# Prompt attention of a hybrid decoder layer: sample columns of a finished head moved into its tile and split with it, one reciprocal and one scaling step for both query tiles of a pair

## The chip, the cores and the metric

The kernel runs on one core of one Trainium2 chip. The metric is the device time of one execution in microseconds; the time quoted for a kernel is the median of its runs. Engines are named as the profile names them: PE multiplies matrices, PEld loads its weights, DVE is the vector engine, ACT the scalar engine, POOL is GpSimd, and SP issues most of the DMAs.

## The reference

One layer of a decoder with two batches at once: a prompt of 1024 new tokens, and 8 sample sequences of 8 new tokens each that attend to 4096 cached positions in pages. Both go through the same stages: a projection, attention over the 256 keys that an indexer picks, a gated recurrence (RG-LRU), a merge of the two branches, an output projection and a SwiGLU FFN. All is float32. Of the attention, per query block of 128:

```python
sel = index_topk(qi, wi, ki, pos, 256)
logits = einsum(q, k_sel) * HEAD_DIM ** -0.5 + rel_bias[rel_bucket(dist)]
p = softmax(where(valid, logits, NEG_INF))
out = einsum(p, v_sel)                       # 8 heads, 2 kv heads, head_dim 128
...
merged = sigmoid(ga) * (attn_out @ w_o_attn) + sigmoid(gb) * (lru_out @ w_o_lru)
```

## The kernel before

Every float32 product is made of three products in a faster format: an operand x is split into hi, which is x rounded to that format, and lo, which is x minus hi. The helper `split` does this with one ACT copy (L194) and one subtraction on DVE or POOL (L198); `mm3` (L181 to L183) multiplies hi by hi, lo by hi and hi by lo into one PSUM bank. The engines' instructions are not run in the order of the code: the tile framework reorders each engine's queue by its own estimate of when operands and buffers are ready, and what it built is then fixed. SP, too, has one queue in order.

The code around the change is `prompt_attention`, a generator that yields after each small step. It runs from about 835 to 1090 us of the span, in two stretches:

- **First stretch, 835 to 988 us.** The attention of the samples (`sample_attention`) runs on all engines, with K and V gathered by POOL's DMAs (L1156), transposed (L1188), copied out of PSUM by ACT and DVE as `kt` (L1190, L1192), multiplied (L1200), and so on. Between its steps the prompt attention is advanced. The flag `self.sdone` is false.
- **Second stretch, 988 to 1090 us.** The samples are done, `self.sdone` is true, and the prompt attention has the core to itself. Heads 0 to 2 and a part of head 3 fall into the first stretch, the rest of the 8 heads into the second. At its end `merge` begins, whose first product reads all heads as weights and streams through the gate of `w_o_attn`.

A head has 8 query tiles of 128 rows, t = 0 to 7, taken as four pairs m = 0 to 3 (`both`). For one tile, `stage_a` adds bias and mask of the nearest 256 keys into E (L1403, on POOL for even t and on DVE for odd t), makes the logits on PE, adds and takes the maximum on DVE out of PSUM into the tile L (L1425, then the reduction L1430), and takes the exponential of L in place on ACT with its row sums (L1431). Tile t has (t + 1) * 128 columns, so 128 to 1024. L1431 is followed by the function `norm`: the reciprocal of the row sums on DVE (L1434) and the scaling of L by it in place, on ACT in the first stretch (L1436) and on POOL in the second (L1438). `norm` isn't run at once but put into the list `nlag = Lag(1)`: the one of tile t is issued when tile t + 1 has been put.

`stage_b` of a pair transposes the scaled L of both tiles on PE (L1499), splits the transposes (`ph` on ACT, `pl` on DVE, both out of PSUM) and multiplies them with V. It is interleaved by `weave` with `both` of a later pair: of the pair two later in the first stretch (PLW) and of the pair four later in the second (PLAG). When a head is through, its output is in DRAM (`atd`), written in four pieces `ao`. In the second stretch `load_at(h)` loads it back as the tile `at` of 1024 columns and splits it into `ah` and `al`, the weights of `merge`; the 64 columns of the samples for that head lie in the constant tile `as_` and are split on their own (`split_s`) into columns 1024 to 1087 of `ah` and `al`. Head 7 isn't written out, and its sample columns are split by `split_s` before its loop. `todo` is a list of postponed steps that `do()` runs at the start of the next pair.

`m()` gives a small tile from a ring of 14. `sqrt_table` (L309) is a one-element square root into such a tile, issued by the later stage `up_init` so that ACT has the table for its square roots before it needs them (L298).

## Time and profile before

| | us |
|---|---|
| median of 3 runs | 2012.59 |
| lowest and highest | 2010.61, 2012.98 |
| the profiled execution's own time | 2007.54 |
| its span (first to last instruction) | 2005.8 |
| prompt attention in it | about 835 to 1090 |

The profile is of one execution. Its span is what the rows below are measured from: a start of 902.77 is 902.77 us after the first instruction. 1.74 us of the execution lie outside of the span. The execution was 5.05 us shorter than the median of the runs, so rows of it are used for differences, not for the level.

### The profile page before, as it was taken

The numbers are of one execution on the slowest core, as the hardware profiler recorded it, in microseconds if no ns is written. First come the engines' busy times: TensorE is split into PE (matmuls) and PEld (weight loads), VectorE is DVE, ScalarE is ACT, GpSimd is POOL, SyncE is SP. The second block draws the span as 40 slices with busy tenths as digits, with TensorE's granted clock in tenths as the row PEclk, the third lists the DMA queues.
The fourth block names the chain that finished last, engine by engine and source line by source line (L and its number), as shares of the span: only waits on it lengthen the run. The fifth ranks groups of instructions, "written<-read, shape, count | busy, mean of one in ns | idle before, by whom it ended". The sixth has DMA issues, their size and how long they took to land.

```text
span 2005.8 us, 33491 instructions
## 1 busy us (share of the span) xinstructions
PE 1934.0 (96%) x12413; PEld 1707.0 (85%) x12413; DVE 1382.7 (69%) x3084; ACT 1014.9 (51%) x1885; POOL 432.2 (22%) x366
## 2 busy tenths in 40 slices
PE   7999999999998989999889999999999999999998
PEld 5999888899997877777688999978888888878886
DVE  6454876788898666577796244596666766586796
ACT  5554688667776332477575122553333333345445
POOL 2102655000002666644474440000000000000000
PEclk9999999999999999999999999999999999999999
DMA  4633444222325998988624325313332332492543
GB/s 144 156 85 100 127 140 122 61 61 79 90 72 190 323 327 298 299 275 265 230 83 170 98 100 182 109 57 107 102 96 84 121 103 90 140 374 86 155 118 106
DMA packets 221152, 297.12 MB, mean 148 GB/s; under 512 B 20228, under 2 KB 155292, under 8 KB 220860
## 3 DMA queue, kind: packets, MB, share of 16 engines
q1 hardware_dynamic: 199484, 219.47, 34.5%
q0 software_dynamic: 21504, 75.51, 10.9%
q8 instruction: 98, 1.61, 0.4%
q14 instruction: 66, 0.54, 0.1%
HBM read 225.51 MB, written 64.28 MB: 144 GB/s over the span
## 4 chain that ended last, share of the span: by engine, by line
PE 73%; DVE 12%; ACT 6%; DMA 4%; issue 3%; POOL 0%; SPq 0%; DVEq 0%; ACTq 0%; POOLq 0%
PE mm L181 9%; PE mm L182 9%; PE mm L183 9%; PE ax L1818 5%; PE ax L1819 5%; PE ax L1820 5%; PE ax L1188 2%; PE mm L1818 2%; PE mm L1819 2%; PE mm L1820 2%; PE mm L2062 2%; PE mm L2061 2%; PE mm L2063 2%; PE ax L1200 2%; PE ax L2062 1%
## 5 line engine op out<-in xcount | busy, mean ns | idle before, releaser
L181 PE MATMUL mm<-xh,wh 128*128 128x384 f32 (+2 forms) x936 | 310.2, 331 | 0.2 <-ACT sg L966 0.2
L183 PE MATMUL mm<-xh,wl 128*128 128x384 f32 (+2 forms) x936 | 307.9, 329 | 0.7 <-POOL wl L198 0.7
L182 PE MATMUL mm<-xl,wh 128*128 128x384 f32 (+2 forms) x936 | 307.8, 329 | 0.0
L183 PEld LDWEIGHTS mm<-xh,wl 128*128 128x128 f32 (+1 forms) x936 | 175.4, 187 | 2.6 <-POOL wl L198 1.5
L181 PEld LDWEIGHTS mm<-xh,wh 128*128 128x128 f32 (+1 forms) x936 | 175.8, 188 | 1.9 <-ACT sg L966 0.7
L194 ACT ACTIVATE wh<-wr 128x1024 fp32r<-128x1024 f32 (+1 forms) x81 | 85.3, 1054 | 181.0 <-PE mm L182 87.8
L182 PEld LDWEIGHTS mm<-xl,wh 128*128 128x128 f32 (+1 forms) x936 | 175.8, 188 | 1.3
L198 POOL TENSOR_TENSOR wl<-wr,wh 128x1024 fp32r<-128x1024 f32 (+1 forms) x47 | 115.5, 2458 | 247.7 <-ACT wh L194 208.2
L1156 POOL DMA_INDIRECT g<-cache_k,c x64 | 69.4, 1085 | 333.0 <-DVE r L1030 272.3
L1818 PE MATMUL ax<-xb,wu 128*128 128x512 f32 x336 | 132.3, 394 | 2.0 <-ACT xb L194 2.0
L1819 PE MATMUL ax<-xb,wu 128*128 128x512 f32 x336 | 131.8, 392 | 0.0
L1820 PE MATMUL ax<-xb,wu 128*128 128x512 f32 x336 | 131.5, 391 | 0.0
L753 ACT ACTIVATE c<-sc,p 128x768 int8<-128x768 f32 (+2 forms) x93 | 96.4, 1037 | 12.2 <-DVE p L797 11.1
L194 ACT ACTIVATE wu<-wg 128x512 fp32r<-128x512 f32 x63 | 37.6, 627 | 94.9 <-DVE wg L1683 92.3
L194 ACT ACTIVATE ha<-hr 128x512 fp32r<-128x512 f32 x77 | 48.3, 627 | 72.7 <-PE ax L2063 30.0
L194 ACT ACTIVATE gh<-wg 128x1024 fp32r<-128x1024 f32 x44 | 46.7, 1061 | 71.0 <-PE ax L1820 37.4
L749 DVE TENSOR_SCALAR_CACHE_REDUCE c<-sc,p 128x384 uint8<-128x384 f32 (+3 forms) x102 | 78.1, 766 | 1.8
L1818 PE MATMUL mm<-xb,gh 128*128 128x512 f32 x200 | 77.9, 393 | 0.7 <-ACT gh L194 0.7
L1820 PE MATMUL mm<-xb,gl 128*128 128x512 f32 x200 | 78.1, 390 | 0.1
L1819 PE MATMUL mm<-xb,gh 128*128 128x512 f32 x200 | 78.0, 391 | 0.0
L181 PE MATMUL mm<-lh,wh 128*128 128x272 f32 x256 | 76.9, 302 | 0.0
L1818 PEld LDWEIGHTS ax<-xb,wu 128*128 128x128 f32 x336 | 63.8, 190 | 15.1 <-ACT xb L194 2.2
(500 smaller groups left out, 5775.4 us busy)
## 6 DMA issues: line engine op xcount, KB each, us to landing
wr<-w_in SPq DMA_DIRECT2D x40, 512.0 KB
hr<-hd SPq DMA_DIRECT2D x77, 256.0 KB
wg<-w_ffn_gate SPq DMA_DIRECT2D x44, 256.0 KB
wg<-w_ffn_up SPq DMA_DIRECT2D x44, 256.0 KB
wd<-w_ffn_down SPq DMA_DIRECT2D x22, 512.0 KB
hd<-hs SPq DMA_DIRECT2D x33, 256.0 KB
x<-x_prompt SPq DMA_DIRECT2D x16, 512.0 KB
wr<-w_o_lru SPq DMA_DIRECT2D x16, 512.0 KB
```

Of the source, the lines that this page charges most:

```text
L181: t.matmul(out, ah, bh, start=start, stop=False)
L182: t.matmul(out, ah, bl, start=False, stop=False)
L183: t.matmul(out, al, bh, start=False, stop=stop)
L194: nc.scalar.activation(hi, src, AF.Copy)
L198: eng.tensor_tensor(out=lo, in0=src, in1=hi.bitcast(F32), op=ALU.subtract)
L749: self.tc.keep_in_program_order(v.tensor_scalar(self.junk[:, :ap.shape[-1]], ap, th, 0.0, op0=op, op1=ALU.add, accum_out=cnt[:, r, i:i + 1]))
L753: self.tc.keep_in_program_order(nc.scalar.activation(self.junka[:, :ap.shape[-1]], ap, AF.Sign, bias=ncd[:, r:r + 1].bitcast(F32), accum_o ...
L1156: nc.gpsimd.indirect_dma_start(out=G[:, :1024], out_offset=None, in_=src, in_offset=bass.IndirectOffsetOnAxis(ap=self.ix32[:, b, c:c + 1], ...
L1818: t.matmul(ps, h[:, c], x[:, :512], start=start and k == 0, stop=False, skip_group_check=True)
L1819: t.matmul(ps, h[:, c], x[:, 512:1024], start=False, stop=False, skip_group_check=True)
L1820: t.matmul(ps, l[:, c], x[:, :512], start=False, stop=k == 3, skip_group_check=True)
L2062: t_.matmul(banks[t], s[:, c], m[:, 512:], start=False, stop=False, skip_group_check=True)
```

## The change

Three things are done. First, `load_at` loads the 64 sample columns of a head with a second DMA, out of `as_` into columns 1024 to 1087 of `at`, and one split over 1088 columns replaces the two over 1024 and 64; the split is put on `todo`, so it comes with the next `do()`. `split_s` is left for head 7 alone. Second, the row sums of a pair's two tiles are the two columns of one small tile `sm`, from a ring of its own (`sr`, 10 buffers), and `norm` is one function for the pair: one reciprocal of 128x2, then the scaling of both tiles. It is put into `nlag` once for a pair, so it is issued after the next pair's second exponential. Third, only the negated maximum still takes a tile of the ring of 14. After the heads, one more `do()` runs what is left on `todo`.

```diff
--- before.py
+++ after.py
@@ -1375,9 +1375,10 @@
         def load_at(h):
             x = self.S(name="at")
             self.dma(x[:, :TP], self.atd[h])
+            self.dma(x[:, TP:NT], self.as_[:, h, :])
+
             self.ah[h], self.al[h] = self.S(F32R, name="ah"), self.S(F32R, name="al")
-            self.split(x[:, :TP], self.ah[h][:, :TP], self.al[h][:, :TP], "s", "v")
-            split_s(h)
+            todo.append(lambda: self.split(x[:, :NT], self.ah[h][:, :NT], self.al[h][:, :NT]))
 
         def split_s(h):
             self.split(self.as_[:, h, :], self.ah[h][:, TP:NT], self.al[h][:, TP:NT])
@@ -1393,7 +1394,7 @@
 
             todo.append(fn)
 
-        def stage_a(h, t):
+        def stage_a(h, t, sm):
             qh, ql = qn[h]
             (kh, kl), _, bt = G[h // 4]
             W = (t + 1) * P
@@ -1426,23 +1427,25 @@
                                            op0=ALU.add, op1=ALU.max, accum_out=mx[:, i:i + 1])
                     i += 1
                 yield
-            nm, sm, rs = self.m(), self.m(), self.m()
+            nm = self.m()
             v.tensor_reduce(nm, mx[:, :i], axis=AX.X, op=ALU.max, negate=True)
             nc.scalar.activation(L[:, :W], L[:, :W], AF.Exp, bias=nm, accum_out=sm)
+            return L
+
+        def both(h, m):
+            sm, rs = (self.m(2, tag="sr", bufs=10) for _ in range(2))
+            La = yield from stage_a(h, 2 * m, sm[:, 0:1])
+            Lb = yield from stage_a(h, 2 * m + 1, sm[:, 1:2])
 
             def norm():
                 self.tc.keep_in_program_order(v.reciprocal(rs, sm))
-                if not self.sdone:
-                    nc.scalar.activation(L[:, :W], L[:, :W], AF.Copy, scale=rs)
-                else:
-                    nc.gpsimd.tensor_tensor(out=L[:, :W], in0=L[:, :W], in1=rs.to_broadcast([P, W]), op=ALU.mult)
+                for L, W, r in ((La, (2 * m + 1) * P, rs[:, 0:1]), (Lb, (2 * m + 2) * P, rs[:, 1:2])):
+                    if not self.sdone:
+                        nc.scalar.activation(L[:, :W], L[:, :W], AF.Copy, scale=r)
+                    else:
+                        nc.gpsimd.tensor_tensor(out=L[:, :W], in0=L[:, :W], in1=r.to_broadcast([P, W]), op=ALU.mult)
 
             nlag.put(norm)
-            return L
-
-        def both(h, m):
-            La = yield from stage_a(h, 2 * m)
-            Lb = yield from stage_a(h, 2 * m + 1)
             return h, m, La, Lb
 
         def weave(a, na, b, nb):
@@ -1545,6 +1548,7 @@
         self.mk = self.MK = None
         while ready:
             load_at(ready.pop(0))
+        do()
 
 
     def merge(self):
```

Line numbers after line 1378 are higher by 1 to 4 in the changed kernel: its reciprocal is L1441, its ACT scaling L1444, its transposes L1502, its exponential L1432.

The order of the instructions moves at three places. The first is ACT in the first stretch, around the exponential of tile 7 of head 1 (the third time in the loop of that kind: L with 1024 columns). `kt` and `run` and the L of L1233 belong to the samples. Before:

```order
L1431 ACTIVATE L_9997,m_10059<-L_9997,m_10058 128x896
L1436 ACTIVATE L_9899<-L_9899,m_9990 128x768
L1232 ACTIVATE run_10050<-run_9921,run_10049 128x1
L1233 ACTIVATE L_10046,m_10048<-L_10046,run_10049 128x512
L194 ACTIVATE ph_10078<-ax_10074 128x384
L1487 ACTIVATE ao_10089<-ax_10082 128x256
L1190 ACTIVATE kt_10118<-ax_10126 128x512
L1190 ACTIVATE kt_10119<-ax_10151 128x512
L1431 ACTIVATE L_10067,m_10145<-L_10067,m_10144 128x1024
L1436 ACTIVATE L_9997<-L_9997,m_10060 128x896
L194 ACTIVATE ph_10173<-ax_10168 128x512
L1431 ACTIVATE L_10161,m_10227<-L_10161,m_10226 128x128
```

and after the change, from the same exponential of 896 columns on:

```order
L1432 ACTIVATE L_9977,sr_9973<-L_9977,m_10038 128x896
L1232 ACTIVATE run_10030<-run_9900,run_10029 128x1
L1233 ACTIVATE L_10026,m_10028<-L_10026,run_10029 128x512
L1490 ACTIVATE ao_10065<-ax_10058 128x256
L1190 ACTIVATE kt_10094<-ax_10102 128x512
L1432 ACTIVATE L_10043,sr_9973<-L_10043,m_10120 128x1024
L1444 ACTIVATE L_9841<-L_9841,sr_9838 128x640
L1444 ACTIVATE L_9878<-L_9878,sr_9838 128x768
L1190 ACTIVATE kt_10095<-ax_10126 128x512
L1432 ACTIVATE L_10138,sr_10134<-L_10138,m_10203 128x128
L194 ACTIVATE ph_10150<-ax_10145 128x512
L194 ACTIVATE ph_10166<-ax_10161 128x512
```

The scalings of 640 and 768 columns now follow each other behind the exponential of 1024 columns; before, they stood behind the exponentials of 768 and 896, and the scaling of 896 columns stood where these are now. On PE, the transposes of the tiles with 640 and 768 columns, which read what ACT scales there, stood like this before:

```order
L182 MATMUL mm_10237<-l_8725,qh_9679 128x256
L1499 MATMUL ax_10168<-c_75,L_9858 128x128
L1499 MATMUL ax_10168<-c_75,L_9899 128x128
L1499 MATMUL ax_10168<-c_75,L_9858 128x128
L1499 MATMUL ax_10168<-c_75,L_9899 128x128
L181 MATMUL ax_10177<-ph_10009,h_8993 128x256
L182 MATMUL ax_10177<-pl_10010,h_8993 128x256
```

and stand like this now:

```order
L183 MATMUL mm_10210<-h_8724,ql_9664 128x256
L1502 MATMUL ax_10145<-c_75,L_9841 128x128
L181 MATMUL ax_10154<-ph_9989,h_8993 128x256
L182 MATMUL ax_10154<-pl_9990,h_8993 128x256
L183 MATMUL ax_10154<-ph_9989,l_8994 128x256
L181 MATMUL ax_10154<-ph_9989,h_8993 128x256
L182 MATMUL ax_10154<-pl_9990,h_8993 128x256
L183 MATMUL ax_10154<-ph_9989,l_8994 128x256
L1502 MATMUL ax_10145<-c_75,L_9878 128x128
L1502 MATMUL ax_10145<-c_75,L_9841 128x128
```

The first transpose of the tile with 768 columns stands behind six products of the pair before it. On DVE, in the same place, two copies `kt` (L1192) stood ahead of the reduction (L1430) that the exponential of 1024 columns waits for; they now stand behind it.

The second place is DVE in the second stretch, at the end of head 4, with the split of the loaded head 2. Before:

```order
L1430 TENSOR_REDUCE m_11973<-mx_11931 128x1
L198 TENSOR_TENSOR pl_12004<-ax_11999,ph_12003 128x384
L1434 RECIPROCAL m_11923<-m_11922 128x1
L1403 TENSOR_TENSOR e_12020<-bt_11546,mk_8981 128x256
L198 TENSOR_TENSOR al_11983<-c_6488,ah_11982 128x64
L198 TENSOR_TENSOR al_11983<-at_11980,ah_11982 128x1024
L1425 ISA L_11992,mx_11993<-mm_11994,e_11990 128x128
L1425 ISA mx_11993 128x1
L1425 ISA L_12022,mx_12023<-mm_12024,e_12020 128x256
L1425 ISA mx_12023 128x1
L1430 TENSOR_REDUCE m_12013<-mx_11993 128x1
L198 TENSOR_TENSOR pl_12056<-ax_12050,ph_12055 128x512
```

and now:

```order
L1431 TENSOR_REDUCE m_11911<-mx_11869 128x1
L1441 RECIPROCAL sr_11726<-sr_11725 128x2
L198 TENSOR_TENSOR pl_11942<-ax_11937,ph_11941 128x384
L1404 TENSOR_TENSOR e_11954<-bt_11503,mk_8981 128x256
L198 TENSOR_TENSOR al_11921<-at_11917,ah_11920 128x1088
L1426 ISA L_11930,mx_11931<-mm_11932,e_11928 128x128
L1426 ISA mx_11931 128x1
L1426 ISA L_11956,mx_11957<-mm_11958,e_11954 128x256
L1426 ISA mx_11957 128x1
L1431 TENSOR_REDUCE m_11951<-mx_11931 128x1
L198 TENSOR_TENSOR pl_11991<-ax_11985,ph_11990 128x512
L1431 TENSOR_REDUCE m_11963<-mx_11957 128x1
```

The small subtraction of 64 columns is gone, the large one has 64 columns more, and there is one reciprocal of two columns for a pair.

The third place is the end of the second stretch on ACT, around the last exponential. Before:

```order
L194 ACTIVATE ph_12945<-ax_12941 128x384
L194 ACTIVATE ph_12968<-ax_12964 128x384
L1431 ACTIVATE L_12912,m_12956<-L_12912,m_12955 128x1024
L194 ACTIVATE ph_12983<-ax_12978 128x512
L194 ACTIVATE ah_13139<-at_13137 128x1024
L1487 ACTIVATE ao_12993<-ax_12928 128x256
L194 ACTIVATE ph_13000<-ax_12996 128x384
L194 ACTIVATE ah_12636<-ax_13004 128x256
L309 ACT_TABLE_LOAD
L309 ACTIVATE m_14575<-c_76 128x1
L194 ACTIVATE ph_13018<-ax_13013 128x512
L194 ACTIVATE ah_13147<-c_6488 128x64
```

and now:

```order
L194 ACTIVATE ph_12867<-ax_12863 128x384
L309 ACT_TABLE_LOAD
L309 ACTIVATE m_14472<-c_76 128x1
L1432 ACT_TABLE_LOAD
L1432 ACTIVATE L_12811,sr_12756<-L_12811,m_12854 128x1024
L194 ACTIVATE ph_12882<-ax_12877 128x512
L194 ACTIVATE ah_12547<-ax_12903 128x256
L1490 ACTIVATE ao_12892<-ax_12827 128x256
L194 ACTIVATE ph_12899<-ax_12895 128x384
L194 ACTIVATE ph_12917<-ax_12912 128x512
```

The one-element square root of `sqrt_table` with its table load has moved ahead of the last exponential, for which the table of the exponential is loaded again; a third table load now stands ahead of the first square root of the output projection (L298). PE has, in the same place, before:

```order
L183 MATMUL ax_13022<-ph_12983,l_11597 128x256
L181 MATMUL ax_13022<-ph_12983,h_11596 128x256
L182 MATMUL ax_13022<-pl_12984,h_11596 128x256
L183 MATMUL ax_13022<-ph_12983,l_11597 128x256
L181 MATMUL ax_13022<-ph_13000,h_11596 128x256
L181 MATMUL mm_13167<-ah_11646,wh_8734 128x384
L1499 MATMUL ax_13029<-c_75,L_12766 128x128
L1499 MATMUL ax_13029<-c_75,L_12821 128x128
```

and now:

```order
L181 MATMUL ax_12903<-ph_12867,h_11550 128x128
L182 MATMUL ax_12903<-pl_12868,h_11550 128x128
L183 MATMUL ax_12903<-ph_12867,l_11551 128x128
L181 MATMUL mm_13064<-ah_11598,wh_8734 128x384
L182 MATMUL mm_13064<-al_11599,wh_8734 128x384
L183 MATMUL mm_13064<-ah_11598,wl_8735 128x384
L181 MATMUL mm_13064<-ah_11603,wh_8734 128x384
L182 MATMUL mm_13064<-al_11604,wh_8734 128x384
L183 MATMUL mm_13064<-ah_11603,wl_8735 128x384
L181 MATMUL mm_13064<-ah_11920,wh_8734 128x384
L182 MATMUL mm_13064<-al_11921,wh_8734 128x384
L183 MATMUL mm_13064<-ah_11920,wl_8735 128x384
```

The first of these products of `merge` (mm out of ah, al and wh, wl) were spread singly among the last transposes; now twelve of them (three for each of the first four heads, the last three right behind this piece) stand together ahead of the transposes of the tiles with 640 and 768 columns of head 7.

## Rows read from the trace of the kernel before

**Rows 1.** Busy time by stretch: start and end, length, then busy time (and instructions) of PE, PEld, DVE, ACT and POOL, the granted clock of PE as a share of full speed, the busy share of the DMA engines and GB/s.

```profile
835.00:988.00 153.00, 145.39 (x1568) 114.68 (x1568) 116.66 (x402) 101.01 (x229) 74.66 (x83) 1.00 0.84 277
988.00:1076.00 88.00, 79.33 (x598) 72.16 (x597) 82.56 (x297) 64.06 (x146) 58.49 (x53) 1.00 0.24 77
1076.00:1090.00 14.00, 11.78 (x99) 11.08 (x98) 11.19 (x19) 10.14 (x20) 3.54 (x2) 1.00 0.65 247
1090.00:1240.00 150.00, 150.00 (x1040) 150.00 (x1039) 50.02 (x86) 30.48 (x49) 50.30 (x39) 1.00 0.36 122
```

**Rows 2.** Waits of PE in 988 to 1082 us: who waited for whom, us in total, times, longest.

```profile
PE mm L181 <- DVE mx L1425: 4.3, 6, 1.4
PE ax L1499 <- DVE pl L198: 2.8, 3, 1.2
PE ax L182 <- DVE pl L198: 1.4, 1, 1.4
```

**Rows 3.** ACT in order of time in the first stretch, head 1: start, length, engine, line, operation, operands, and in brackets the idle time ahead of it with what ended it.

```profile
892.12 0.81 ACT L1436 ACTIVATE L<-L,m 128x640 f32<-128x640 f32 x1
...
898.52 0.92 ACT L1436 ACTIVATE L<-L,m 128x768 f32<-128x768 f32 x1
...
904.03 1.15 ACT L1431 ACTIVATE L<-L,m 128x1024 f32<-128x1024 f32 x1 [1.04 <-DVE m L1430]
905.17 1.03 ACT L1436 ACTIVATE L<-L,m 128x896 f32<-128x896 f32 x1
906.11 0.57 ACT L194 ACTIVATE ph<-ax 128x512 fp32r<-128x512 f32 x1
```

**Rows 4.** PE in order of time at the same place.

```profile
902.77 0.60 PE L1499 MATMUL ax<-c,L 128*128 128x128 f32 x4
...
907.46 1.06 PE L1200 MATMUL ax<-kt,c 128*32 128x512 f32 x8 [1.33 <-DVE pl L198]
```

**Rows 5.** DVE in order of time at the same place.

```profile
902.65 1.28 DVE L1192 COPY kt<-ax 128x512 f32<-128x512 f32 x2
903.85 0.14 DVE L1430 TENSOR_REDUCE m<-mx 128x1 f32<-128x3 f32 x1
```

**Rows 6.** DVE in 988 to 1082 us by line and shape: count, busy time, mean ns of one, idle time before.

```profile
L198 DVE TENSOR_TENSOR al<-at,ah 128x1024 fp32r<-128x1024 f32 x6 | 8.7, 1448 | 0.6 <-ACT ah L194 0.6
L198 DVE TENSOR_TENSOR al<-c,ah 128x64 fp32r<-128x64 f32 x7 | 5.9, 837 | 0.0
L1434 DVE RECIPROCAL m<-m 128x1 f32<-128x1 f32 x37 | 5.7, 154 | 2.2 <-ACT L L1431 2.2
```

**Rows 7.** DVE in order of time at the start of the second stretch.

```profile
1000.50 0.15 DVE L1434 RECIPROCAL m<-m 128x1 f32<-128x1 f32 x1
1000.58 0.67 DVE L198 TENSOR_TENSOR pl<-ax,ph 128x512 fp32r<-128x512 f32 x1
1001.17 1.67 DVE L198 TENSOR_TENSOR al<-c,ah 128x64 fp32r<-128x64 f32 x1
...
1006.39 0.21 DVE L198 TENSOR_TENSOR al<-c,ah 128x64 fp32r<-128x64 f32 x1
1006.52 0.42 DVE L1403 TENSOR_TENSOR e<-bt,mk 128x256 f32<-128x256 f32 x1
```

**Rows 8.** POOL in order of time at the same place.

```profile
1001.08 1.67 POOL L1438 TENSOR_TENSOR L<-L,m 128x896 f32<-128x896 f32 x1
...
1010.26 2.25 POOL L1438 TENSOR_TENSOR L<-L,m 128x1024 f32<-128x1024 f32 x2 [2.31 <-DVE m L1430]
```

**Rows 9.** All engines in order of time in 1020 to 1026 us, of which ACT's split of the loaded head 2 and DVE's.

```profile
1022.16 1.70 DVE L198 TENSOR_TENSOR al<-c,ah 128x64 fp32r<-128x64 f32 x1
1022.44 1.04 ACT L194 ACTIVATE ah<-at 128x1024 fp32r<-128x1024 f32 x1
...
1023.78 1.21 DVE L198 TENSOR_TENSOR al<-at,ah 128x1024 fp32r<-128x1024 f32 x1
```

**Rows 10.** PE in order of time at the start of the second stretch.

```profile
1012.21 1.20 PE L1499 MATMUL ax<-c,L 128*128 128x128 f32 x9 [1.12 <-POOL L L1438]
```

**Rows 11.** ACT in order of time at the end of the second stretch.

```profile
1075.66 1.15 ACT L1431 ACTIVATE L<-L,m 128x1024 f32<-128x1024 f32 x1 [0.26 <-DVE m L1430]
...
1076.81 0.58 ACT L194 ACTIVATE ph<-ax 128x512 fp32r<-128x512 f32 x1
...
1078.87 0.39 ACT L194 ACTIVATE ah<-ax 128x256 fp32r<-128x256 f32 x1
1079.28 1.28 ACT L309 ACT_TABLE_LOAD   x1
1080.57 0.20 ACT L309 ACTIVATE m<-c 128x1 f32<-128x1 f32 x1
```

**Rows 12.** PE in order of time at the end of the second stretch and at the start of `merge`.

```profile
1078.84 0.63 PE L1499 MATMUL ax<-c,L 128*128 128x128 f32 x4 [1.17 <-DVE pl L198]
...
1081.47 0.66 PE L1499 MATMUL ax<-c,L 128*128 128x128 f32 x4 [1.00 <-DVE pl L198]
...
1083.73 0.60 PE L1499 MATMUL ax<-c,L 128*128 128x128 f32 x4
...
1090.56 0.34 PE L181 MATMUL mm<-ah,wh 128*128 128x384 f32 x1
1090.74 0.33 PE L182 MATMUL mm<-al,wh 128*128 128x384 f32 x1
```

## The prediction

> **What bounds the kernel now.** I read the busy time by stretch first [rows 1]. In each line the reader sets the busy time of PE against the length: what is left is all that any edit at that place can give. From 1090 us on PE is busy for 150.00 of 150 us at a granted clock of 1.00, and the order there is nearly the same in both kernels, so nothing behind 1090 us can gain. Ahead of it PE is idle for 7.61 us in the first stretch, 8.67 us from 988 to 1076 and 2.22 us in the 14 us after. The change can thus win 18.5 us at most, 0.92% of the time, while it has no such limit on the other side. PE bounds the first stretch (145.39 of 153 us). In the second DVE is the busiest beside it: 82.56 us in the 88 us, and what PE waits for there is DVE: 4.3, 2.8 and 1.4 us in the three largest groups, 8.5 us together [rows 2]. So a microsecond of work taken from DVE between 988 and 1076 us can be worth a microsecond, and one taken from any engine elsewhere is worth what PE waits for it.
>
> **The change, part by part: the first stretch.** Here the pair's scaling is what moves. Before, the tile with 640 columns was scaled at 892.12 (0.81 us) and the one with 768 at 898.52 (0.92 us) [rows 3], and their first transposes ran at 902.77 [rows 4]: PE had 3 us and more in hand. Now both scalings stand behind the exponential of 1024 columns, which began at 904.03 after a wait of 1.04 us for the reduction L1430. That reduction came at 903.85, behind two kt copies of 1.28 us [rows 5], and stands ahead of them now. So the exponential can start when ACT is free, at 904.03 - 1.04 = 902.99, and ends 1.15 us later; the two scalings end at about 904.96 and 905.9. The first transpose can't run before 904.96. From 902.77 to 907.46 PE worked for 4.69 - 1.33 = 3.36 us, since 1.33 us of it was a wait ahead of L1200 [rows 4]; that wait was for pl, whose ph began on ACT at 906.11, behind the scaling of 896 columns at 905.17 [rows 3], and that scaling is gone from there. If all of the 3.36 us waits for the first transpose, PE is at the same point at 904.96 + 3.36 = 908.32 instead of 907.46: 0.86 us lost. Three heads are here, so 3 x 0.86 = **+2.6 us**. Bounds: if the exponential stays at 904.03, the transposes wait 1.04 us more, 1.9 us a head, so +5.7 in all; if other products fill PE's gap ahead of the first transpose (six now stand between the transposes of the two tiles), the gap hides behind them and the old wait of 1.33 us ahead of L1200 is won; I bound that by one such win in the three heads, -1.3. I take the middle case because the order shows PE's transposes still at the head of that piece.
>
> **The second stretch.** DVE had 37 reciprocals there in 5.7 us [rows 6]; half of them go. One costs the queue less than its 0.15 us: at 1000.50 it ran, and the next started at 1000.58, so 0.08 us from start to start [rows 7]. 18.5 x 0.08 = -1.5 us. Seven small subtractions of 64 columns go. Where nothing disturbed one it took 0.21 us and the next instruction started 0.13 us after it (1006.39 to 1006.52) [rows 7]: 7 x 0.13 = -0.9. The large subtractions get 64 more columns each; at 1.21 us for 1024 [rows 9] that is 0.08 us each, +0.5 for seven. Together **-1.9 us**.
>
> The small subtractions took 5.9 us, though, a mean of 837 ns against 209 alone: 4.4 us more than 7 x 0.21 [rows 6]. The row at 1001.17 shows why: 1.67 us for 64 columns, ended at 1002.84, just after the scaling of 896 columns on POOL that began at 1001.08 and ended at 1002.75 [rows 7, 8]. It waited inside for POOL. The Trainium skill, "SBUF — State Buffer", section "Who interferes with whom", has this as a rule: a DVE instruction with two SBUF inputs contends with a GpSimd instruction that reads SBUF, and the lock is exclusive and lasts for the whole instruction of the one that came first. The trace agrees here (1.67 against 0.21 us), and by the rule alone the wait belongs to POOL's work, which this change doesn't shorten, and would pass to the next instruction of that kind. What the trace itself shows on that: behind the small subtraction the order has the large one, whose operands lie in the same places, and at 1023.78 it could only start after the small one (1022.16, 1.70 us) and after ah of 1024 columns on ACT (1022.44 + 1.04 = 1023.48) [rows 9]; without the small one it would have come 0.3 us earlier, not 1.70. So I take 0 of the 4.4 us, and keep -4.4 as the end of the range.
>
> At the turn from the first stretch to the second PE waited 1.12 us for POOL's scaling, at 1012.21 [rows 10]; POOL had begun it at 1010.26 after waiting for the same reduction as everyone [rows 8]. One scaling more falls to POOL and one fewer to ACT, and the order of the transposes there leaves the tile more time: I take half, **-0.6**, between 0 and -1.1. Sum of the stretch -2.5, between 0 and -6.9; more than the 8.67 us of idle time it can't be.
>
> **The end of the stretch.** The square root's table load (1.28 us) and its 0.20 us, which stood at 1079.28 behind everything [rows 11], now stand ahead of the last exponential (1075.66), with another load of 1.28 us after them. 1.28 + 0.20 + 1.28 = 2.76 us, of which 0.26 us were idle: the next ph comes 2.5 us later than 1076.81. Before, PE waited there for pl of such a ph, 1.17 us ahead of 1078.84, and once more 1.00 us ahead of 1081.47, just behind the table load [rows 12]. The second wait goes with the load. Into the first, now 1.17 + 2.5 = 3.7 us, twelve products of merge have been moved, 0.18 us each from start to start (1090.56 to 1090.74) [rows 12]: 2.1 us. Idle time 3.7 - 2.1 = 1.6 instead of 2.17: -0.6. Against it, the last exponential is 2.5 us late, and the scalings of the last pair on POOL follow it; the transposes of that pair ran at 1083.73, and if the scalings end after that, PE waits again. I take **0**, between -1.5 and +2.8 (all of the two loads paid).
>
> **At nothing:** seven more DMAs of 64 columns on SP, into tiles that wait for a load of 1024 columns anyway; eight fewer small copies on ACT, which is busy for 64.06 of 88 us [rows 1]; the third table load, which stands after 1090 us, where PE is busy all the time and ACT 30.48 of 150 us [rows 1]. If ACT were late there, it would cost its 1.28 us.
>
> **Sum:** +2.6 - 2.5 + 0 = +0.1 us. The profiled execution would go from 2007.54 to 2007.6 us. It lay 5.05 us below the median of 2012.59, so only the difference is carried over: **2012.7 us**.
>
> **The rivals.**
>
> A, slower: the scalings are late everywhere. The exponential of 1024 columns doesn't come earlier, the transposes wait 1.9 us a head in the first stretch (+5.7), and in the second DVE's saved time gives nothing, because a pair that is scaled in one go on POOL is later for its first tile, and PE waits for POOL as it did at 1012.21. It decides from the point where PE's waits for the scaling, over all heads, exceed what DVE gives back by 4 us. For it: 3 us in hand became none in the first stretch [rows 3, 4]. Against it: in the second stretch the transposes follow four pairs later. 2012.59 + 5.7 = 2018.3.
>
> B, faster: the waits inside the small subtractions don't pass on. Then the second stretch has its full -6.9, and with +2.6 the sum is -4.3: 2008.3. For it: not each is followed by one that reads two SBUF tensors; the one at 1000.58 read PSUM and took 0.67 us beside no scaling [rows 7]. Against it: the large subtraction that follows in the order, and POOL's unchanged work.
>
> C, a switch of tables costs twice its row. In the trace the load at 1079.28 stands 0.02 us behind the end of the instruction before it (1078.87 + 0.39) and the next starts when it ends, at 1080.57 [rows 11]: no delay beside it. If the delay were there and as long as the load, the end would go from 0 to +2.6: 2012.7 + 2.6 = 2015.3. The Trainium skill, "ScalarE: Activation LUTs", section "What ACT_TABLE_LOAD costs", states such a delay: about 1283 ns for the load and 1380 ns of draining, 2.66 us for each switch. The row agrees with the load and shows no draining.
>
> D, the change does nothing where PE waits, since the freed time of DVE was idle time and the moved scalings are covered: 2012.6.
>
> **How the numbers follow.** What a measurement of this kernel can tell from no change is about 0.2%, 4.0 us. Forecast 0.44, A 0.22, B 0.26, C 0.05, D 0.03. Faster by more is B: 0.26. Slower is A: 0.22. Within are the forecast, C and D: 0.52. The forecast's own range is 2009 to 2016.5. The range that should hold 8 in 10 takes in A and B with a part of the bounds: from 2006.0 (B, with the first stretch at about its zero) to 2018.5 (A). The sum of all lower ends (-1.3 - 6.9 - 1.5) and of all upper ones (5.7 + 0 + 2.8) lie outside of it, as they'd have to come together.
>
> **What would show it.** In the profile after: a wait of PE's transposes for ACT's scaling behind the exponential of 1024 columns, about 0.9 us in each of three heads, shows the first term; PE's idle time of the first stretch should be near 10 us instead of 7.61. In the second stretch there should be about 18 reciprocals and no subtraction of 64 columns; if the mean of the large ones rises above 1448 ns, the waits have passed on, if it stays and PE's idle time falls from 8.67 to under 4 us, B is right. At the end: a load, a square root and a load ahead of the last exponential, and PE's idle time from 1076 to 1090 us near 2.2 us. The end of the prompt attention, where PE becomes busy without a gap, should stay within 1 us of 1090. Wrong would be the whole if times behind that point changed, where the order is the same.

## The result, and the profile after

| | before | after |
|---|---|---|
| median of 6 runs, us | 2011.06 (2009.96 to 2012.98) | 2022.92 (2016.82 to 2026.1) |
| ratio, 95% interval | | 1.0055, 1.0041 to 1.0068 |
| span of the profiled execution, us | 2005.8 | 2019.7 |

The change costs 11.9 us where +0.1 was forecast, and 2022.92 lies above the range. It went the way of rival A, further than priced.

Three points of the program are the same in every kernel: the first exponential of the prompt attention, the last transposes of the samples (L1249), and the first product of `merge` with 320 columns, behind which the order is the same. Between the first two lies the first stretch, between the last two the second and its end. The windows view of PE at these points, for the kernel before in a second execution, profiled later (the first had 150.45 and 110.53 us): start and end, length, PE's busy time and instructions, granted clock, share of the DMA engines, GB/s.

```profile
839.55:990.03 150.48, 142.85 (x1555) 1.00 0.85 280
990.03:1100.55 110.52, 99.59 (x742) 1.00 0.35 123
```

And for the changed kernel:

```profile
837.80:997.74 159.94, 145.37 (x1555) 0.98 0.78 264
997.74:1111.94 114.20, 103.52 (x742) 0.97 0.31 110
```

The first stretch is 9.5 us longer: PE's idle time (length less busy time) is 14.57 instead of 7.63 us, and its busy time 2.5 us more at a mean clock of 0.98. The rest is 3.7 us longer, with idle time as before (10.68 against 10.93) and 3.9 us more busy time at 0.97. Behind it nothing differs: from there to the end of the span it is 907.76 us after and 907.95 before. The prompt attention itself began 0.9 us later.

What PE waits for in the first stretch (us in total, times, longest), after the change:

```profile
PE ax L1502 <- ACT L L1444: 8.5, 5, 2.6
PE ax L1502 <- ACT kt L1190: 2.4, 4, 0.7
```

The first line had no counterpart before. PE in order of time, these five waits:

```profile
848.57 0.84 PE L1502 MATMUL ax<-c,L 128*128 128x128 f32 x3 [0.90 <-ACT L L1444]
...
858.10 0.33 PE L1502 MATMUL ax<-c,L 128*128 128x128 f32 x1 [0.97 <-ACT L L1444]
...
869.66 0.47 PE L1502 MATMUL ax<-c,L 128*128 128x128 f32 x1 [2.15 <-ACT L L1444]
...
911.17 0.33 PE L1502 MATMUL ax<-c,L 128*128 128x128 f32 x1 [1.93 <-ACT L L1444]
...
951.78 0.47 PE L1502 MATMUL ax<-c,L 128*128 128x128 f32 x1 [2.58 <-ACT L L1444]
```

The last three are the transposes behind the exponential of 1024 columns, in heads 0, 1 and 2; they answer to the row at 902.77 of [rows 4], which had no wait. ACT at the first of them:

```profile
867.64 1.15 ACT L1432 ACTIVATE L<-L,m 128x1024 f32<-128x1024 f32 x1 [0.19 <-DVE m L1431]
868.79 1.64 ACT L1444 ACTIVATE L<-L,sr 128x640 f32<-128x640 f32 x2
```

The transposes start where the scaling of 640 columns ends, inside these 1.64 us. In head 1 the same exponential waited for the reduction, and DVE ahead of that for PE's own logits:

```profile
908.15 0.43 DVE L1426 CUSTOM_DVE_ANT_0 L<-mm,mk 128x256 f32<-128x256 f32 x1 [1.16 <-PE mm L183]
909.16 1.15 ACT L1432 ACTIVATE L<-L,m 128x1024 f32<-128x1024 f32 x1 [1.54 <-DVE m L1431]
```

And the clock around it, then around 951.78 and at the turn to the second stretch, in steps of 2 us (columns as above):

```profile
866.00:868.00 2.00, 1.50 (x12) 1.00 0.94 281
868.00:870.00 2.00, 0.34 (x2) 0.83 0.97 385
870.00:872.00 2.00, 2.00 (x11) 0.50 1.02 408
872.00:874.00 2.00, 2.00 (x16) 0.82 0.51 207
...
950.00:952.00 2.00, 0.22 (x2) 0.81 0.95 358
952.00:954.00 2.00, 2.00 (x11) 0.50 1.03 410
954.00:956.00 2.00, 2.00 (x15) 0.84 0.71 289
...
998.00:1000.00 2.00, 1.33 (x21) 0.76 0.51 205
1000.00:1002.00 2.00, 2.00 (x33) 0.50 0.03 8
1002.00:1004.00 2.00, 2.00 (x9) 0.50 0.00 0
1004.00:1006.00 2.00, 2.00 (x9) 0.54 0.05 11
```

Behind the standstill PE runs at half of its 2.4 GHz for a while, which is called half clock from here on. Length times what is missing to 1.00 gives its price: 2 x (0.17 + 0.50 + 0.18) = 1.7 us at the first place, 1.7 at the second, 2 x (0.24 + 0.50 + 0.50 + 0.46) = 3.4 at the third. This is an upper bound, since PE stands still in a part of that time: in the first stretch it sums to 3.4 us, and PE's busy time rose by 2.5. The kernel before shows no half clock from 835 to 1240 us in either execution [rows 1].

In the second stretch PE now waits for POOL, and DVE's rows are smaller where they were meant to be:

```profile
PE ax L1502 <- POOL L L1446: 4.1, 5, 1.2
PE mm L181 <- DVE mx L1426: 1.6, 3, 0.7
```

```profile
L198 DVE TENSOR_TENSOR al<-at,ah 128x1088 fp32r<-128x1088 f32 x5 | 8.1, 1618 | 2.5 <-ACT ah L194 2.5
L1441 DVE RECIPROCAL sr<-sr 128x2 f32<-128x2 f32 x19 | 2.9, 153 | 3.4 <-ACT L L1432 3.4
L198 DVE TENSOR_TENSOR al<-c,ah 128x64 fp32r<-128x64 f32 x1 | 0.2, 198 | 0.0
```

Against [rows 6] the reciprocals fell from 37 to 19 (5.7 to 2.9 us) and the small subtractions from 7 to 1 (5.9 to 0.2 us). PE's waits for DVE fell, from the 4.3 us of [rows 2] to 1.6 in the first group, and those for POOL rose from the 1.12 us of [rows 10] to 4.1.

### The profile page after: what moved, and what is told of

Read it like the earlier page. It is cut to its first block, busy times and chain, and to the rows that moved or that the text cites. A ratio compares the mean times of both kernels' runs of the same rounds, so it can differ in the third digit from the quotient of the medians.

```text
span 2019.7 us, 33471 instructions
## 1 busy us (share of the span) xinstructions
PE 1939.6 (96%) x12413; PEld 1710.4 (85%) x12413; DVE 1375.5 (68%) x3045; ACT 1017.6 (50%) x1879; POOL 434.7 (22%) x367
## 4 chain that ended last, share of the span: by engine, by line
PE 45%; DVE 3%; ACT 2%; DMA 1%; issue 1%; POOL 0%; ACTq 0%; SPq 0%; DVEq 0%; POOLq 0%
PE ax L1822 5%; PE ax L1823 5%; PE ax L1824 5%; PE mm L181 3%; PE mm L182 3%; PE mm L183 3%; PE mm L1822 2%; PE mm L1823 2%; PE mm L1824 2%; PE mm L2066 2%; PE mm L2067 2%; PE mm L2065 2%; PE ax L2066 1%; PE ax L2067 1%; PE ax L2065 1%; PE mm L189 1%
## 5 line engine op out<-in xcount | busy, mean ns | idle before, releaser
L753 ACT ACTIVATE c<-sc,p 128x768 int8<-128x768 f32 (+2 forms) x93 | 96.4, 1037 | 12.2 <-DVE p L797 11.1
```

The source lines that it names most:

```text
L753: self.tc.keep_in_program_order(nc.scalar.activation(self.junka[:, :ap.shape[-1]], ap, AF.Sign, bias=ncd[:, r:r + 1].bitcast(F32), accum_o ...
```

## The experiments

Theory T: the loss of the first stretch is the place of the scaling on ACT, right ahead of its reader, and the half clock behind the longest waits. Rivals: R1, the loads and splits; R2, the pairing, two scalings in one go; R3, the second stretch loses by itself. Lengths of the two stretches, from the windows view at the points named above, and PE's idle time in the second (length less busy time, so the clock is not in it):

| run | first, us | second, us | PE idle in the second, us | ratio to before, 95% interval |
|---|---|---|---|---|
| kernel before, two executions | 150.45, 150.48 | 110.53, 110.52 | 10.9, 10.9 | |
| changed kernel | 159.94 | 114.20 | 10.7 | 1.0055, 1.0041 to 1.0068 |
| the same, e16 | 158.57 | 112.76 | 9.8 | 1.0062, 1.0041 to 1.0083 |
| e1, e12: loads alone | 150.48, 150.41 | 107.93, 108.79 | 7.4, 6.2 | 0.9988, 0.9970 to 1.0006; 0.9990, 0.9973 to 1.0007 |
| e2: pairs alone | 161.61 | 120.01 | 15.2 | 1.0077, 1.0049 to 1.0105 |
| e3: scaled one tile earlier | 150.78 | 113.88 | 11.1 | 1.0014, 0.9997 to 1.0031 |
| e4: pairs in the second stretch alone | 150.95 | 114.02 | 9.6 | 1.0012, 0.9995 to 1.0028 |
| e11: the same, one tile earlier | 150.95 | 115.01 | 11.4 | 1.0025, 1.0012 to 1.0039 |
| e14: pairs from head 5 | 150.94 | 109.80 | 7.7 | 0.9996, 0.9983 to 1.0009 |
| e13: single, but late | 154.30 | 110.57 | 10.9 | 1.0008, 0.9992 to 1.0024 |
| e9: before, reader later | 158.36 | 114.11 | 9.3 | 1.0040, 1.0026 to 1.0054 |
| e10: changed, reader later | 158.43 | 117.14 | 9.8 | 1.0077, 1.0056 to 1.0098 |

**Halves of the change.** e1 is before with the new `load_at` and the last `do()`, e2 is before with the new `both` and `norm`; e12 is e1 once more.

> The kernel before with the first part of the change alone (sample columns loaded into the tile, one split of 1088 columns put on the list of postponed steps, the last do()). The scaling stays as before. Theory T (the loss is PE's wait for the pair's late scaling on ACT, 8.5 us in the changed kernel's first stretch, and the half clock after the longest waits): nothing of that is in here, so PE idles about 7.6 us from 835 to 988 as before, the granted clock stays at 1.00, and the time is within 0.2% of before, with a gain of 0 to 2 us if the seven subtractions of 64 columns were worth anything. Rival R1 (the loss comes from the loads and splits of the finished heads): 5 us or more slower.

> The kernel before with the second part alone (one reciprocal and one scaling step for both tiles of a pair, put on the lag list once for a pair); load_at and its two splits as before. Theory T: all of the loss, 9 to 13 us slower, with four or five waits of the transposes for the scaling in the first stretch, 7 to 9 us together, and stretches of half clock behind those over 2 us. Rival R1: within 3 us of before.

> The first part of the change alone, once more, beside the run above: its first run was 0.12% faster than before with an interval that reached over 0. Theory T: again 0 to 0.3% faster, PE's idle time of the second stretch about 2 us below before.

R1 falls: the loads alone leave the first stretch as it was and shorten the second by 2.6 and 1.7 us. The gain in time, 0.1% twice, isn't clear of zero. The pairs alone have all of the loss, with the same five waits (8.5 us). In the second stretch they lose more than the whole change does: 120.01 us, with 15.2 us idle. With the loads it is 114.20 and 10.7, so there the loads give back a part of what the pairs cost.

**The place of the scaling.** e3 is the changed kernel with the pair's step issued one exponential earlier:

```diff
             nc.scalar.activation(L[:, :W], L[:, :W], AF.Exp, bias=nm, accum_out=sm)
+            if pn:
+                pn.pop(0)()
...
-            nlag.put(norm)
+            pn.append(norm)
```

> The changed kernel, but the pair's reciprocal and both scalings are issued after the next pair's first exponential, not its second; pairing, splits and loads as in the changed kernel. Theory T (it is the place of the scaling that costs): the transposes' waits for ACT in the first stretch fall from 8.5 us to under 2, no half clock there, and the time is 7 us or more below the changed kernel's 2022.9, at 2010 to 2016. Rival R2 (it is the two scalings back to back, 1.6 us of ACT at once, that hold up the evictions): waits of PE for ACT stay, 2018 or more.

The scalings of 640 and 768 columns still stand back to back in heads 0 and 2, as here in head 0,

```profile
861.12 1.64 ACT L1446 ACTIVATE L<-L,sr 128x640 f32<-128x640 f32 x2
```

and the first stretch is 150.78 us, without a wait for the scaling among its seven largest groups and without half clock. So R2 falls here: with the reader where it is, it is the one exponential more that costs. e13 does the reverse to the kernel before, single scalings but later:

```diff
-        pend, nlag = [], Lag(1)
+        pend, nlag = [], Lag(2)
...
                     while not self.sdone:
                         yield
+                    nlag.n = 1
+                    nlag.q.pop(0)()
```

> The kernel before (single reciprocals, single scalings, both splits of a load), but in the first stretch a tile's scaling is issued two exponentials later instead of one; the second stretch is as before. Theory T (lateness costs, not pairing): the tile with 640 columns is scaled behind the exponential of 896 columns and the one with 768 behind that of 1024, so PE's transposes of that pair wait for ACT again, 3 to 7 us in the first stretch, 3 to 9 us slower than before. Rival R2 (pairing costs): within 0.2% of before.

The first stretch is 3.8 us longer without any pair, all of it idle time, of which 2.1 us in three waits is for the scaling itself:

```profile
PE ax L1200 <- DVE pl L198: 2.5, 2, 1.7
PE ax L1499 <- ACT L L1436: 2.1, 3, 0.9
```

None of these waits is over 0.9 us and the clock stays at 1.00; the second stretch is 110.57. The time, +0.08%, is not clear of zero, and only the stretch decides for T. The waits are smaller than expected since the first tile of the pair is scaled one exponential earlier than in the changed kernel.

**The place of the reader.** The changed kernel with `PLW = 3` in place of 2, on two chips, and the control, before with `PLW = 3`.

> The changed kernel with the scaling where it is, but the transposes of a pair come one pair later in the first stretch (three pairs behind instead of two). Theory T says that the late scaling costs only since its reader stands right behind it: the transposes' waits for ACT fall from 8.5 us to under 2, no half clock in the first stretch, 7 us or more faster than the changed kernel. Rival R2 (the two scalings back to back hold up ACT's other work): the time stays within 3 us of the changed kernel, with waits for kt and ph in place of those for the scaling.

> The kernel before with nothing changed but that the transposes of a pair come one pair later in the first stretch (three pairs behind instead of two). It is the control for the run in which the same was done to the changed kernel and the time didn't fall. If putting the readers later costs by itself (the waits for kt of the samples that showed there, 7.3, 4.5 and 4.2 us), this one is as far above before as that run was, 0.7% or more, and says that the late scaling's cost was really gone there. If it is within 0.2% of before, the paired scaling holds ACT up in another way than by its reader, as rival R2 says.

> The changed kernel with the transposes one pair later in the first stretch, once more, beside its control on one chip. Theory T: within 0.3% of the control, waits of the transposes for ACT's scaling under 2 us. R2: 0.5% or more above the control.

The run e7 missed: 1.0105 (1.0081 to 1.0129) beside 1.0073 for the changed kernel, with the waits for the scaling down to 1.0 us. (That chip took 2058.92 us for the kernel before; runs e5 to e8 are compared with each other alone.) The control shows that the later reader costs by itself, but 0.40% and not the 0.7% set for T. In time e10 was 0.37% above its control, between the bounds set for T and R2. The first stretches of the control and of e10 are equally long:

```profile
841.52:999.88 158.36, 142.79 (x1516) 0.96 0.81 265
837.43:995.86 158.43, 139.94 (x1515) 0.99 0.81 264
```

That they are equal is in part chance. In the control PE is idle for 15.6 us, and half clock sums to 6.8 us; in e10 it is 18.5 and 1.7, and PE's waits for ACT's kt add up to 11.3 us against 6.0, as R2 would have it. So these runs don't decide between T and R2; e3 and e13 do, with the reader in its place. (Some 40 of PE's instructions also move from the first stretch into the second here, so the lengths are compared with each other alone.) The second stretch of e10 is longer, 117.14 against 114.11; 1.7 us of the difference are half clock.

**The half clock.** e8 adds work ahead of the reader; e5 is the changed kernel beside it.

```diff
+                if m == 2 and j0 == 0 and not self.sdone:
+                    for _ in range(14):
+                        nc.tensor.transpose(pt[:, :P], self.ident, self.ident)
```

> The changed kernel once more, as it is, so that the next three can be set beside it on one chip: again 0.4 to 0.8% slower than before, the same waits of the transposes for ACT in the first stretch (8 to 9 us), and half clock behind those over 2 us.

> The changed kernel with 14 transposes of the identity added ahead of the first transpose of the pair with 640 and 768 columns, in the three heads of the first stretch; they are overwritten and do nothing but keep PE busy, some 0.12 us each from start to start, 1.6 us in each head. The order also lets six to ten products of the pair before pass ahead of the transposes in two of the heads. Theory T, with its second part (the clock falls to half because PE stands still for over 2 us): no half clock in the first stretch, PE's idle time there 6 us or more lower and its busy time 5 us higher, and the time 3 to 6 us below the changed kernel although work was added. If the clock has nothing to do with the standstill, half clock shows at the same places, and the time stays within 2 us of the changed kernel or rises by up to 5.

The first stretch of e5, then of e8:

```profile
856.42:1050.77 194.35, 156.65 (x1560) 0.94 0.65 217
857.97:1049.37 191.40, 158.57 (x1596) 0.97 0.66 220
```

In e5 the waits for the scaling were 13.5 us, more than the 8 to 9 expected. In e8 they fell to 3.6 us, half clock from 12.1 to 5.1 us (what is left of it stands at waits for kt), and the stretch took 191.40 us instead of 194.35 though work was added. The medians are 2071.27 and 2073.03, with ratios of 1.0051 (1.0034 to 1.0068) and 1.0073 (1.0047 to 1.0099). The direction is T's, the size under the 3 us expected and not clear of noise. Since products of another pair moved ahead of the transposes as well, the run doesn't tell the shorter waits from the clock.

**The second stretch.** e4 scales tile by tile while the samples run and by pairs after; e11 is e4 with the pair's step one exponential earlier and the square root held; e14 is e4 with pairs for heads 5 to 7 alone. `norm1` is the old `norm` of one tile.

```diff
             nc.scalar.activation(L[:, :W], L[:, :W], AF.Exp, bias=nm, accum_out=sm)
+            if not self.sdone:                # e14: or h < 5
...
+                nlag.put(norm1)
+            else:                             # e11 alone
+                nlag.flush()
...
-            nlag.put(norm)
+            if self.sdone:                    # e14: and h >= 5
+                nlag.put(norm)
```

> The changed kernel with the scaling tile by tile, each behind the next tile's exponential, as long as the samples run, and by pairs only after them. Theory T: the first stretch is as before (PE idle 7 to 8 us, clock 1.00), the second as in the changed kernel without its half clock (idle 10 to 11 us against 10.9 before): within 4 us of before. Rival R3 (the second stretch loses by itself, since PE's transposes wait for POOL's pair, 4.1 us in the changed kernel): 2015 or more.

> What theory T would build of the change: loads and splits as changed, scaling tile by tile in the first stretch, by pairs in the second but issued behind the next pair's first exponential, and the square root held in its place. Theory T: first stretch as before, and in the second POOL's pair comes one tile earlier, so PE's waits for POOL fall from 4.1 us to under 2.5 and DVE's saved time (5 us) reaches PE: 1 to 4 us faster than before, at or below the run with the loads alone. If the second stretch's gain is lost to pairing whatever its place (R3), it is slower than the run with the loads alone by 2 us or more.

> The changed kernel with tile by tile scaling up to head 4 and pairs for heads 5 to 7 alone, behind the next pair's second exponential. If pairs cost only at the turn, where the transposes follow less than four pairs behind, PE's waits for POOL (4.1 us) are gone and the time is that of the loads alone, 0 to 4 us faster than before. If they cost in every head, 3 us or more are lost against the loads alone, so it is at before or above.

In time e4 stayed within the 4 us that T gave (2014.28 us beside 2011.79 for the kernel before), and its first stretch is that of before. T's build e11 missed: its waits for POOL fell to 1.7 us, as expected, but it is 0.25% slower than before. With pairs from the turn on, early or late, the second stretch takes 114 to 115 us, against 108 to 109 for the loads alone. A part of that is half clock, summed in steps of 1 us as above: 5.1 us in e4, 3.4 in e11, 3.4 in the changed kernel, so 108.9, 111.6 and 110.8 without it. Taken off whole, it is too much by up to 2.5 us: the second run of the loads alone, e12, has 3.4 us in its 108.79, so 105.4, and the first has none in its 107.93. PE's idle time doesn't have this uncertainty. In order, the second stretch of e1, e4, e11 and e14:

```profile
989.65:1097.58 107.93, 100.56 (x742) 1.00 0.35 122
991.45:1105.47 114.02, 104.45 (x742) 0.96 0.32 111
992.23:1107.24 115.01, 103.61 (x743) 0.97 0.34 119
994.97:1104.77 109.80, 102.15 (x743) 0.98 0.33 115
```

PE is idle for 6.2 to 7.4 us with the loads alone and for 9.6 to 11.4 with pairs from the turn on (e3, e4, e11 and the changed kernel). Pairs that begin at head 5 (e14) have 7.7, no wait of PE for POOL among the groups down to 0.4 us, and a time between the loads alone and before. That looks as if pairs cost at the turn alone, where few pairs lie between a scaling and its reader (two when it begins, four later). But they cost in later heads as well, by a way that T doesn't have. POOL also adds bias and mask for the even tiles (L1404). Behind a pair of 896 and 1024 columns this addition comes late, and DVE stands still for it. POOL and then DVE in the changed kernel, in head 6:

```profile
1057.26 3.58 POOL L1446 TENSOR_TENSOR L<-L,sr 128x896 f32<-128x896 f32 x2 [0.96 <-ACT L L1432]
1060.81 0.67 POOL L1404 TENSOR_TENSOR e<-bt,mk 128x256 f32<-128x256 f32 x1
...
1061.51 0.42 DVE L1426 CUSTOM_DVE_ANT_0 L<-mm,e 128x256 f32<-128x256 f32 x1 [1.05 <-POOL e L1404]
```

In the whole second stretch these waits of DVE come to 0.4 us in each of the six profiles without pairs there (before twice, e1, e9, e12, e13), to 2.4 us in e14, where two heads have one, and to 3.4 to 5.2 us in all others, one in each of three heads. From the exponential of 1024 columns of head 5 to that of head 6, all engines as in [rows 1], for the loads alone, e14 and the changed kernel:

```profile
1039.70:1057.49 17.79, 17.61 (x134) 16.47 (x134) 17.56 (x64) 13.93 (x33) 14.15 (x14) 1.00 0.24 70
1044.97:1063.80 18.83, 18.24 (x135) 16.77 (x135) 16.58 (x60) 13.95 (x34) 14.95 (x13) 1.00 0.22 66
1051.56:1070.89 19.33, 18.14 (x135) 16.68 (x134) 17.74 (x61) 13.96 (x33) 15.25 (x13) 1.00 0.22 67
```

This head costs 1.0 to 1.5 us more with pairs, at full clock. At the turn itself PE's new waits for POOL's scaling stand largely in place of others: from the turn to the exponential of 1024 columns of head 5 PE is idle for 6.9 us in the changed kernel, 6.0 and 4.8 with the loads alone, and 7.6 before. They go where the reader stands one pair further behind at the turn: PE doesn't wait for POOL's scaling at all in e7 and e10. So R3 holds: pairs cost in the second stretch by themselves, and in the later heads in the way that R2 gave for ACT, but on POOL. Whether its half clock belongs to them is open, as told below.

**The table loads.** The changed kernel with the square root kept in program order:

```diff
-        self.nc.scalar.activation(self.m(), self.epsd, AF.Sqrt)
+        self.tc.keep_in_program_order(self.nc.scalar.activation(self.m(), self.epsd, AF.Sqrt))
```

> The changed kernel with the one-element square root held in its place, so that its table load stands behind the last exponential and the second and third loads are gone. By the prediction's term for the end of the stretch (0, between -1.5 and +2.8) nothing is won: within 2 us of the changed kernel, PE's idle time at the end of the prompt attention within 1 us of it. Rival C (a switch costs twice its row): 2.5 to 5 us faster than the changed kernel.

In the run the square root stands behind the first square root of the output projection, whose load stays; the two loads around the last exponential are gone. It took 2074.87 us (ratio 1.0082, 1.0054 to 1.0110) beside 2073.03 for e5, and its second stretch 112.04 us (1.7 of it half clock) beside 111.33: nothing is won that could be seen, as the prediction's term said, though the times alone can't exclude the lower end of rival C. The loads in the changed kernel, ACT in order of time:

```profile
1090.32 1.28 ACT L309 ACT_TABLE_LOAD   x1
1091.62 0.20 ACT L309 ACTIVATE m<-c 128x1 f32<-128x1 f32 x1
1091.84 1.28 ACT L1432 ACT_TABLE_LOAD   x1
1093.13 1.15 ACT L1432 ACTIVATE L<-L,m 128x1024 f32<-128x1024 f32 x1
```

Each is followed within 0.02 us; rival C, a delay beside the load, isn't there.

**Both kernels once more.**

> The kernel before, as it is, for a second profile. If half clock at the turn is chance that follows the standstill of 1.45 and 0.68 us which every kernel has there, it may show here too; if it comes with the change, the granted clock stays at 1.00 from the last sample transposes on, as in its first profile, and the stretch from there to the first product of 320 columns takes 110.5 us again.

> The changed kernel once more, for another profile and time beside those: 0.4 to 0.8% slower than before, 9 to 11 us more than before in the first stretch, half clock behind the waits of the exponential of 1024 columns in heads 0 and 2, and again at the turn if that comes with the change.

Before repeats to 0.03 us in both stretches. The changed kernel had half clock again, behind the wait in head 2 and at the turn, not in head 0; its first stretch was 8.1 us longer than before, with 6.7 us more idle time, a little under the 9 to 11 expected.

## Why the prediction failed, step by step

- **First stretch, the step that failed.** The wait itself was sized well: the scaling to end at 904.96 where PE stood ready at 902.77 means 2.19 us, and 2.15, 1.93 and 2.58 us were measured. But I set the wait of 1.33 us ahead of L1200 against it and multiplied the difference by three. That wait stands once in the whole stretch, in head 1 [rows 4]; heads 0 and 2 had nothing to win. 3 x 2.19 - 1.33 = 5.2 us would have been the term, not 2.6. Two waits of 0.9 us in head 0, behind the shorter pairs, were not looked for. Together the idle time rose by 6.9 us. That 2.19 us fits so well is in part luck: I let the exponential start as soon as ACT is free, but in head 1 ACT stood idle for 1.54 us until the reduction came, behind PE's own logits.
- **The clock, a term that was missing.** I took PE's rows at 1.00 as fixed and priced standstill by its length. Two of the new waits were followed by half clock at up to 1.7 us each, and PE's busy time rose by 2.5 us in the first stretch. With the idle time this makes the 9.5 us.
- **Second stretch.** That DVE is relieved was right, and of the 4.4 us inside the small subtractions I took too little: e1 won 2.6 us there, e12 1.7. Part of the wait did pass on: in e1 the additions of bias and mask on DVE (L1404, two SBUF inputs) took 853 ns each, 18 of them, against 732 before, so 2.2 us. This agrees with the Trainium skill, "SBUF — State Buffer", section "Who interferes with whom": a DVE instruction with two SBUF inputs contends with a GpSimd instruction that reads SBUF. Before, then e1:

```profile
L1403 DVE TENSOR_TENSOR e<-bt,mk 128x256 f32<-128x256 f32 x18 | 13.1, 732 | 0.0
L1404 DVE TENSOR_TENSOR e<-bt,mk 128x256 f32<-128x256 f32 x18 | 15.3, 853 | 0.0
```

In the changed kernel the sign that I had set for it shows, too: the large subtractions took 1618 ns instead of 1448. There the gain of the loads is seen only against the pairs alone (10.7 us of idle time instead of 15.2); against before nothing is left of it (10.7 and 10.9), since the pairs cost as much. The wait for POOL at the turn, for which I took -0.6, grew by 3.0 us instead: I had looked at "four pairs later" and not at the turn, where it is two. And one path I put at nothing by leaving it out: two scalings at once hold up POOL's own additions, and DVE, the busiest engine beside PE there, waits 3.0 us more for them (3.45 against 0.45), in three heads. Rival A named both stretches, but in the second only PE's wait for POOL, and its price of 5.7 us lacked the clock. I also took PE's 8.5 us of waits for DVE [rows 2] as lying ahead of 1076; 2.2 us of them, the waits at 1078.84 and 1081.47 [rows 12], lie behind it and stand in the term for the end once more.
- **The end, the extra loads, the DMAs.** 0, as forecast: the last exponential came 2.6 us later relative to its neighbour, and the time behind it was made up, since from its start to the first product of 320 columns it is 18.8 us instead of 22.2.

**What stays open.** Half clock at the turn (3.4 us in the changed kernel, 1.7 in e16) follows a standstill of 1.45 and 0.67 us that the kernel before has as well, at 987.32 and 988.85, without it. Right behind it half clock showed in e2, e4, e7, e8 and e11 as well, all with pairs there, but also in e9 and e14, which scale tile by tile at that point; it didn't in before (twice), e1, e12 and e13, nor in e3, e5, e6 and e10, which have pairs there. The other falls of the second stretch came at other waits: in e16 17 us later, behind one of 1.09 us for POOL and one of 0.88 us for DVE; in e12, without pairs, at one of 2.03 us for DVE. So pairs aren't needed for it, no run shows by what it comes, and up to 3.4 us of the loss aren't traced.

## What to carry to other kernels

A step that is merged with its neighbour moves to where the later of the two can run, and a list that postponed single steps by one then postpones pairs by one: this change lost by that second move, as e3 shows. Look for the reader of the earlier step and price its wait in each place where the loop passes, with a credit only where its row stands. On a PE that is busy nearly all the time a new standstill of 2 us can cost nearly twice its length (2.15 us, and up to 1.7 us of half clock behind it). The distance between a producer and its reader has to be read at the start of a stage as well, where the pipeline is short. And two steps at once hold up what else their engine does: ask who waits for that, too.

## What the hardware showed unexpectedly

Half clock came in pieces that cost 1.7 or 3.4 us, as worked out above, and not always behind the same wait: behind the wait of 2.15 us in the changed kernel and in e2, not in e16; behind 2.6 us in all three; behind 1.93 us in e2 alone. So the length of the standstill alone doesn't decide it, and the 2 us named ahead of e8 are no threshold: the same wait can have half clock behind it in one execution and not in the next, and the price of a wait has this uncertainty.
